# Ordering a layer's ScalarE and VectorE work behind the weight splits, and cutting the layer heads into parts

## The chip, the cores and the metric

The kernel runs on one NeuronCore of a Trainium2 chip. The metric is the device time of one execution in microseconds (us). Before the change the median of three runs is 1137.03 us (1136.1 to 1137.7).

## The reference

Two layers over a 512 x 1024 activation `x`, float32, and a last RMSNorm. Each layer normalizes `x`, projects it with one wide matrix, runs three mixers on column blocks of the result, gates and sums them, and projects back:

```python
h = rmsnorm(x, norm_g)
aq, ak, av, az, buv, bz, cq, ck, cv, cz, gl = split_cols(h @ w_in)
ya = rmsnorm(diff_attention(rope(aq), rope(ak), av, lam), subln_g) * (1 - lam_init) * silu(az)
u, vb = split(gelu(buv)); yb = u * sgu(layernorm(vb)) * silu(bz)      # chunks of 128 positions
yc = dilated_window_attention(rope(cq), rope(ck), cv) * silu(cz)      # three (window, dilation) patterns
pb = einsum('nbsc,ncd->nbsd', [ya, yb, yc], w_branch)
x = x + (sigmoid(gl) * pb).sum(branches) @ w_out
```

`lam` is a scalar of each layer, made from four short vectors (`exp(q1.k1) - exp(q2.k2) + lam_init`).

## The kernel before, in words

**Weights.** A weight is read as a unit of 128 x 1024 float32 by a DMA that SyncE issues (`load`, two `raw` buffers). Each unit is two slots of 128 x 512. A slot is split by `slot`: ScalarE copies it to the rounded type (`whi`, L159), and a subtraction gives the rest (`wlo`, L160), on VectorE, for every fifth slot after the 32nd on GpSimd. There are six `whi` and five `wlo` buffers, so a slot's split waits until the matmuls of the slot six (five) earlier are done. A product is three matmuls (`mm3`: high times high, high times low, low times high), and a slot feeds twelve of 512 columns.

Some pairs of units ("S" groups) go through a seven-product scheme instead: GpSimd and VectorE first form four sums of weight blocks (`t12`, `t34`, L179 to L182), and those are then split like weights. `t12` and `t34` share their two buffers with the probabilities `pr` of the attention.

**Activations.** `x` is split in the same way, into `xh` and `xl`, by `split` (ScalarE L402, VectorE or GpSimd L403), once the norm's scale has been put into `xf` (L555). `mixes` forms eight sums and differences of `x` blocks for the seven-product scheme (`tm`, L475 to L478) and splits them (`mh`, `ml`).

**The order of a layer** is the list of `plan`: `vb` (the gelu half of the gating unit), `val A`, `val C`, then `split`, `mix`, then `pp`, which projects pairs of blocks (q and k of a head, or z), attention A, attention C, `sgu`, the gates and branch products, and `out`. `vb`, `val A` and `val C` are the 512-wide projections (`proj_M`): eight slots each, chunk by chunk of the 1024 inputs. They use an unscaled split of `x` (`xuh`, `xul`). While they run, the head of the layer is prepared: `scale` in `i_vb` (L555, eight instructions), the gelu of `vb` (`gelu2`: L458 to L461), its statistics (L568 to L570), then `i_split` and `i_mix`.

**Banks.** `ps_pj` and `ps_s` have two PSUM banks each and `ps_to` four. A third product in `ps_pj` waits until the first has been read.

**Order on an engine.** Each engine runs its instructions strictly in the order of its queue. The queues are put in order when the program is built: a scheduler takes the instructions with their dependencies and lays them out on a simulated timeline of its own, and weight splits have a raised priority (`PRIO`). `V`, `A`, `G`, `T` are VectorE, ScalarE, GpSimd and TensorE.

Of the kernel before, what the change touches and what calls it, by code (L numbers as in the profile page):

```python
# [16 lines left out]
PSUM = bass.MemoryType.PSUM  # L17

# [13 lines left out]
XLG = (1, 3, 5, 7)  # L32
# [65 lines left out]

@with_exitstack
def hybrid_kernel(ctx: ExitStack, tc, xT, posr, wpack, tabs, cvec, pvec, rvec, lamv, sguw, outT):  # L100
# [264 lines left out]
    lambdas()  # L365
# [161 lines left out]
    def layer(l, xu, parts):  # L527
# [13 lines left out]
        def i_vb():  # L541
# [7 lines left out]
            def scale():  # L549
                bc = rms_spread(norm["rst"])  # L550
                rbc = t2k("sh", name="rbc")
                A.activation(out=rbc, in_=bc, func=AF.Copy)
                for kc in range(KC):
                    xsc = xu.f[kc // 2][:, kc % 2, :]
                    V.scalar_tensor_tensor(  # L555
                        out=xsc, in0=xsc, scalar=ng[:, l, kc : kc + 1], in1=rbc, op0=ALU.mult, op1=ALU.mult
                    )

            banks = [ps_to() for _ in range(4)]
            yield from proj_M(banks, xu.pair, {1: norm_sum, 4: scale})  # L560
            rst = norm["rst"]
            mv = sm.tile([P, 4, 2], F32, tag="mv", bufs=1, name="mv")
            rv = sm.tile([P, 4, 1], F32, tag="rv", bufs=1, name="rv")
            for tb in range(4):
                o = vb[:, tb, :]
                A.activation(out=o, in_=banks[tb], func=AF.Copy, scale=rst[:, tb : tb + 1])
                gelu2(o, o)
                V.bn_stats(out=st[:, tb, :], in_=o)  # L568
                V.bn_aggr(out=mv[:, tb, :], in_=st[:, tb : tb + 1, :])
            V.tensor_scalar(out=rv, in0=mv[:, :, 1:2], scalar1=4.0 * EPS, scalar2=None, op0=ALU.add)  # L570
            G.tensor_tensor(out=rv[:, :, 0], in0=rv[:, :, 0], in1=mhalf, op=ALU.pow)
            sgu["norm"] = mv, rv

        def i_split():
            for kc in range(KC):
                split(xh[:, kc, :], xl[:, kc, :], xu.f[kc // 2][:, kc % 2, :], G if kc in XLG else V)
            return
            yield
# [89 lines left out]
        def i_val(br):  # L668
            if br == BR_A:
                val[br] = v = new_y("va")  # L670
                banks = [ps_pj(), ps_pj(), ps_s(), ps_s()]
                yield from proj_M(banks, xu.pair, {})
# [6 lines left out]
            yield from proj_M(banks, xu.pair, {})  # L679
# [110 lines left out]
        def final(c):  # L790
# [8 lines left out]
            "vb": i_vb, "split": i_split, "mix": i_mix, "vbn": i_vbn, "after": i_after, "u2": i_u2, "bz2": i_bz2, "sgu": i_sgu, "val": i_val, "pp": i_pp, "gl2": i_gl2, "pb": i_pb, "out": i_out,  # L799
# [312 lines left out]
```

## Time and profile before

| | before |
|---|---|
| median of three runs | 1137.03 us |
| profiled execution | 1134.42 us |
| its span, first to last instruction | 1132.7 us |
| mean granted TensorE clock | 0.994 |
| TensorE (PE) busy | 1101.8 us, 97% |
| VectorE (DVE) busy | 815.2 us, 72% |
| ScalarE (ACT) busy | 598.4 us, 53% |
| GpSimd (POOL) busy | 487.8 us, 43% |
| VectorE `wlo` of `raw` (L160) | 261 instructions, mean 820 ns |
| VectorE `wlo` of `t` (L160) | 88 instructions, mean 1070 ns |

PE's busy time is close to the span, so PE sets the time wherever its queue does not wait. What is left, 1132.7 - 1101.8 = 30.9 us, is idle time of PE, at the start, in waits and at the end. The other engines are busy less, but they run in order too, and where one of them is late with something PE needs, PE waits.

### The profile page before, as it was taken

To read this page: it belongs to the slowest core of one execution; us is meant where nothing else is said; L and a number is where in the kernel's file an instruction comes from. 1 tells how busy PE (TensorE), PEld (TensorE's weight loads), DVE (VectorE), ACT (ScalarE), POOL (GpSimd) and SP (SyncE) were. 2 spreads that over 40 slices of the span, in tenths; PEclk is the share of its full clock that TensorE was granted. 3 is DMA by queue.
4 is the path that set the end of the run, shared out by engine and by line. 5 is a ranking of instruction groups with operands and counts; after the bars stand their busy time and mean duration, and the time that the engine had idled before them with its cause. 6 is when DMAs were issued, how large, how long until landed. Compare 5 with 4: busy or idle time off the path is not lost.

```text
span 1132.7 us, 17894 instructions
## 1 busy us (share of the span) xinstructions
PE 1101.8 (97%) x6444; PEld 943.7 (83%) x6444; DVE 815.2 (72%) x1500; ACT 598.4 (53%) x1281; POOL 487.8 (43%) x438
## 2 busy tenths in 40 slices
PE   7799999999998999999999999999999999999996
PEld 5588878877878999998888878788788889999886
DVE  7776777566769888874559578775679787788643
ACT  6654655566765444443546546464757644445330
POOL 4313434432524656663334235524244256657431
PEclk9999999999999999999999999999999999999998
DMA  6242221221213233333622413132203122333433
GB/s 204 73 130 93 69 82 56 93 76 38 75 38 113 89 99 97 109 115 110 223 93 75 130 38 112 39 111 76 75 3 111 56 80 91 111 112 94 138 118 98
DMA packets 35064, 105.97 MB, mean 94 GB/s; under 512 B 4704, under 2 KB 7776, under 8 KB 34976
## 3 DMA queue, kind: packets, MB, share of 16 engines
q1 hardware_dynamic: 29936, 98.50, 27.7%
q10 hardware_dynamic: 5040, 6.34, 1.8%
q8 instruction: 51, 0.84, 0.3%
q14 instruction: 37, 0.30, 0.1%
HBM read 100.58 MB, written 4.24 MB: 93 GB/s over the span
## 4 chain that ended last, share of the span: by engine, by line
PE 86%; DVE 8%; DMA 2%; issue 2%; ACT 1%; POOL 1%; POOLq 0%; SPq 0%; DVEq 0%; ACTq 0%
PE ps_pj L397 15%; PE ps_pj L398 15%; PE ps_pj L399 15%; PE ps_to L397 8%; PE ps_to L399 8%; PE ps_to L398 8%; PE ps_s L823 4%; PE ps_to L862 2%; PE ps_to L424 2%; PE ps_to L968 2%; PE ps_to L893 2%; PE ps_to L422 2%; PE ps_to L423 2%; DVE wlo L160 2%; DVE xf L555 1%
## 5 line engine op out<-in xcount | busy, mean ns | idle before, releaser
L159 ACT ACTIVATE whi<-raw 128x512 fp32r<-128x512 f32 x316 | 193.8, 627 | 254.5 <-DMA raw<-in_wpack 122.7
L160 DVE TENSOR_TENSOR wlo<-raw,whi 128x512 fp32r<-128x512 f32 x261 | 212.1, 820 | 113.9 <-ACT whi L159 36.9
L397 PE MATMUL ps_pj<-xh,whi 128*128 128x512 f32 (+1 forms) x544 | 208.5, 383 | 0.8 <-ACT whi L159 0.5
L398 PE MATMUL ps_pj<-xl,whi 128*128 128x512 f32 (+1 forms) x544 | 206.0, 379 | 0.0
L399 PE MATMUL ps_pj<-xh,wlo 128*128 128x512 f32 (+1 forms) x544 | 205.5, 378 | 0.0
L160 POOL TENSOR_TENSOR wlo<-raw,whi 128x512 fp32r<-128x512 f32 x55 | 76.8, 1397 | 139.1 <-PE ps_pj L399 53.4
L397 PEld LDWEIGHTS ps_pj<-xh,whi 128*128 128x128 f32 x544 | 102.5, 188 | 21.6 <-issue 3.6
L399 PEld LDWEIGHTS ps_pj<-xh,wlo 128*128 128x128 f32 x544 | 102.5, 188 | 19.4 <-issue 2.7
L398 PEld LDWEIGHTS ps_pj<-xl,whi 128*128 128x128 f32 x544 | 102.6, 189 | 18.4 <-issue 2.3
L160 DVE TENSOR_TENSOR wlo<-t,whi 128x512 fp32r<-128x512 f32 x88 | 92.5, 1070 | 16.1 <-ACT whi L159 9.8
L159 ACT ACTIVATE whi<-t 128x512 fp32r<-128x512 f32 x112 | 65.7, 624 | 53.8 <-DVE t L180 35.2
L397 PE MATMUL ps_to<-mh,whi 128*128 128x256 f32 x320 | 91.1, 285 | 1.4 <-DVE zs L507 0.7
L398 PE MATMUL ps_to<-ml,whi 128*128 128x256 f32 x320 | 90.5, 283 | 0.0
L399 PE MATMUL ps_to<-mh,wlo 128*128 128x256 f32 x320 | 90.1, 283 | 0.0
L838 ACT ACTIVATE pr<-pr,nm 128x128 f32<-128x128 f32 (+3 forms) x128 | 70.6, 553 | 32.9 <-DVE nm L834 32.7
L440 POOL TENSOR_TENSOR rsh<-rsh,sinr 128x512 f32<-128x512 f32 x32 | 41.8, 1307 | 105.2 <-DVE rsh L438 95.1
L834 DVE CUSTOM_DVE_ANT_0 pr<-ps_s,tab 128x128 f32<-128x128 f32 (+3 forms) x128 | 57.4, 485 | 28.6 <-PE ps_s L823 26.4
L397 PE MATMUL ps_to<-xh,whi 128*128 128x256 f32 x240 | 68.0, 283 | 0.7 <-ACT whi L159 0.7
L399 PE MATMUL ps_to<-xh,wlo 128*128 128x256 f32 x240 | 67.5, 284 | 1.0 <-DVE wlo L160 1.0
L398 PE MATMUL ps_to<-xl,whi 128*128 128x256 f32 x240 | 67.8, 283 | 0.0
L397 PEld LDWEIGHTS ps_to<-mh,whi 128*128 128x128 f32 x320 | 61.3, 192 | 3.3 <-ACT whi L159 1.6
L399 PEld LDWEIGHTS ps_to<-mh,wlo 128*128 128x128 f32 x320 | 61.1, 192 | 0.6 <-DVE wlo L160 0.4
(241 smaller groups left out, 2864.0 us busy)
## 6 DMA issues: line engine op xcount, KB each, us to landing
raw<-in_wpack SPq DMA_DIRECT2D x174, 512.0 KB
xf<-in_xT SPq DMA_DIRECT2D x8, 256.0 KB
xr<-in_xT ACTq DMA_DIRECT2D x8, 256.0 KB
x1d<-xf SPq DMA_DIRECT2D x8, 256.0 KB
raw<-in_wpack SPq DMA_DIRECT2D x4, 256.0 KB
xr<-x1d ACTq DMA_DIRECT2D x4, 256.0 KB
xr<-x1d ACTq DMA_DIRECT2D x8, 128.0 KB
out<-xf SPq DMA_DIRECT2D x8, 128.0 KB
```

Of the source, the lines that this page charges most:

```text
L159: A.activation(out=hi, in_=src, func=AF.Copy)
L160: (G if made[0] % LOMOD == 0 and made[0] > FIRST_G else V).tensor_tensor(out=lo, in0=src, in1=hi.bitcast(F32), op=ALU.subtract)
L397: T.matmul(ps, lhsT=wh, rhs=mh, start=first, stop=False)
L398: T.matmul(ps, lhsT=wh, rhs=ml, start=False, stop=False)
L399: T.matmul(ps, lhsT=wl, rhs=mh, start=False, stop=last)
L422: T.matmul(banks[tb], lhsT=mh_[:, ts], rhs=wh, start=kc == 0, stop=False)
L423: T.matmul(banks[tb], lhsT=ml_[:, ts], rhs=wh, start=False, stop=False)
L424: T.matmul(banks[tb], lhsT=mh_[:, ts], rhs=wl, start=False, stop=kc == KC - 1)
L440: G.tensor_tensor(out=sh, in0=sh, in1=sinr, op=ALU.mult)
L823: T.matmul(pss[m][:, at[i]], lhsT=q[HALF[m], a, qs], rhs=k[HALF[m], b, :W], start=t == 0, stop=t == 2)
L834: V.tensor_tensor_reduce(out=o, in0=pss[m][:, at[i]], in1=tab[:, 0 if br == BR_A else 1, S - W :], op0=ALU.add, op1=ALU.min, scale=-0.125, ...
L838: A.activation(out=o, in_=o, func=AF.Exp, scale=-1.0, bias=nm[:, m : m + 1], accum_out=den[:, m : m + 1],)
```

## The change

`V` and `A` are wrapped from the first layer on in a class, `Behind`: every ScalarE or VectorE instruction that a layer issues through them gets an ordering dependency, without a semaphore, on the newest plain weight split of its engine at the time it was written (`newest`). It must stand behind that split in the queue. The four splits of a seven-product group (`plain=False`) don't count as newest. The splits of the weights themselves are issued through `nc.scalar` and `nc.vector`.

The head is cut up. `prepare(kc)` is called after each chunk of `val A`: one `xf` scaling, and after every second chunk the gelu and statistics of one block of `vb`. `split_x(kc)` is called after each chunk of `val C`: one split of `x`, all eight now on VectorE (four were on GpSimd). `mix` comes after `val C` as before, but behind the weights. The lambdas of both layers, with their DMA, move from ahead of the layers to the end of `val C` of the first. There are six `wlo` buffers instead of five. In the last layer, three additions of squares move from GpSimd to VectorE. The instructions of TensorE are the same, and their order changes in places.

The diff, with imports and renamings left out:

```diff
-XLG = (1, 3, 5, 7)
-    start = [("vb",), ("val", BR_A), ("val", BR_C), ("split",), ("mix",), ("pp", BR_A, 0)]
+    start = [("vb",), ("val", BR_A), ("val", BR_C), ("mix",), ("pp", BR_A, 0)]
...
+class Behind:
+    def __init__(self, tc, eng, newest, n):
+        self.tc, self.eng, self.newest, self.n = tc, eng, newest, n
+    def __getattr__(self, name):
+        fn = getattr(self.eng, name)
+        def issue(*a, **k):
+            r = fn(*a, **k)
+            self.tc.add_manual_dep(r.ins, self.newest[self.n].name, ORDER, reason="behind the weights")
+            return r
+        return issue
...
+    newest = [None, None]
+    @contextmanager
+    def behind_weights():
+        with tc.issue_after(newest[0]), tc.issue_after(newest[1]):
+            yield
...
-    def slot(src, dst=None):
+    def slot(src, dst=None, plain=True):
...
-            lo = wp.tile([P, S], F32R, tag="wlo", bufs=NSLOT - 1, name="wlo")
+            lo = wp.tile([P, S], F32R, tag="wlo", bufs=NSLOT, name="wlo")
...
+            a = nc.scalar.activation(out=hi, in_=src, func=AF.Copy).ins
+            r = (G if on_g else nc.vector).tensor_tensor(out=lo, in0=src, in1=hi.bitcast(F32), op=ALU.subtract)
+            if plain and dst is None:
+                newest[0] = a
+                if not on_g:
+                    newest[1] = r.ins
...
-                        slot(src)
+                        slot(src, plain=False)
...
-                (V if kc == KC - 1 or self.first else G).tensor_tensor(out=self.ss[:, c], in0=self.ss[:, c], in1=sq[:, c], op=ALU.add)
+                (V if kc == KC - 1 or self.first or c.start else G).tensor_tensor(out=self.ss[:, c], in0=self.ss[:, c], in1=sq[:, c], op=ALU.add)
...
-    lambdas()
...
+        def prepare(kc):
+            xsc = xu.f[kc // 2][:, kc % 2, :]
+            st, mv, rv = sgu["norm"]
+            tb = kc // 2
+            o = sgu["vb"][:, tb, :]
+            with behind_weights():
+                V.scalar_tensor_tensor(
+                    out=xsc, in0=xsc, scalar=ng[:, l, kc : kc + 1], in1=norm["rbc"], op0=ALU.mult, op1=ALU.mult
+                )
+                if kc % 2:
+                    gelu2(o, o)
+                    V.bn_stats(out=st[:, tb, :], in_=o)
+                    V.bn_aggr(out=mv[:, tb, :], in_=st[:, tb : tb + 1, :])
...
+        def split_x(kc):
+            with behind_weights():
+                split(xh[:, kc, :], xl[:, kc, :], xu.f[kc // 2][:, kc % 2, :])
+                if l == 0 and kc == KC - 1:
+                    lambdas()
...
-            mixes(blocks)
+            with behind_weights():
+                mixes(blocks)
...
-                yield from proj_M(banks, xu.pair, {})
+                yield from proj_M(banks, xu.pair, {kc: partial(prepare, kc) for kc in range(KC)})
...
-            yield from proj_M(banks, xu.pair, {})
+            yield from proj_M(banks, xu.pair, {kc: partial(split_x, kc) for kc in range(KC)})
...
+    V, A = Behind(tc, nc.vector, newest, 1), Behind(tc, nc.scalar, newest, 0)
```

**Place 1, VectorE, first layer's head (`val A` runs on TensorE).** `wlo` is a weight's rest, `xf` the scaled `x`, `gw` and `vb` steps of the gelu, `st` the statistics, `xl` the rest of `x`; the numbers tell buffers' uses apart. Before:

```order
L555 SCALAR_TENSOR_TENSOR xf_98<-xf_98,pv_87,rbc_359 128x512 x2
L555 SCALAR_TENSOR_TENSOR xf_104<-xf_104,pv_87,rbc_359 128x512 x2
L555 SCALAR_TENSOR_TENSOR xf_110<-xf_110,pv_87,rbc_359 128x512 x2
L555 SCALAR_TENSOR_TENSOR xf_113<-xf_113,pv_87,rbc_359 128x512 x2
L568 BN_STATS st_257<-vb_254 128x6
L461 SCALAR_TENSOR_TENSOR vb_254<-gth_434,vb_254 128x512
L459 SCALAR_TENSOR_TENSOR gw_442<-gw_442,vb_254 128x512
L459 SCALAR_TENSOR_TENSOR gw_451<-gw_451,vb_254 128x512
L403 TENSOR_TENSOR xl_93<-xf_98,xh_92 128x512
L403 TENSOR_TENSOR xl_93<-xf_104,xh_92 128x512
L403 TENSOR_TENSOR xl_93<-xf_110,xh_92 128x512
L160 TENSOR_TENSOR wlo_416<-raw_337,whi_415 128x512
```

And now, the same stretch (L187 is the weight's subtraction, L110 the wrapper's line):

```order
L187 TENSOR_TENSOR wlo_421<-raw_361,whi_420 128x512
L110 SCALAR_TENSOR_TENSOR xf_98<-xf_98,pv_87,rbc_343 128x512
L187 TENSOR_TENSOR wlo_438<-raw_361,whi_437 128x512
L110 SCALAR_TENSOR_TENSOR xf_98<-xf_98,pv_87,rbc_343 128x512
L110 SCALAR_TENSOR_TENSOR gw_444<-gw_444,vb_238 128x512
L187 TENSOR_TENSOR wlo_465<-raw_395,whi_464 128x512
L110 SCALAR_TENSOR_TENSOR xf_104<-xf_104,pv_87,rbc_343 128x512
L187 TENSOR_TENSOR wlo_482<-raw_395,whi_481 128x512
L110 SCALAR_TENSOR_TENSOR xf_104<-xf_104,pv_87,rbc_343 128x512
L110 SCALAR_TENSOR_TENSOR gw_488<-gw_488,vb_238 128x512
L110 SCALAR_TENSOR_TENSOR vb_238<-gth_445,vb_238 128x512
L187 TENSOR_TENSOR wlo_509<-raw_441,whi_508 128x512
```

Before, fifteen instructions of the head stand together ahead of `wlo_416`. Now a `wlo` stands behind every one to three of them.

**Place 2, VectorE, from `val C` to the first `pp` of the first layer.** `vs` is the eviction of `val C`, `rsh` and `t1` are the two readers of the first `pp` bank (`ps_pj_803`), `ml` rests of the mixes, `neglam` the lambdas. Before:

```order
L160 TENSOR_TENSOR wlo_741<-raw_676,whi_740 128x512
L685 SCALAR_TENSOR_TENSOR vs_746<-ps_to_609,rp_303,vs_746 128x8x64
L160 TENSOR_TENSOR wlo_817<-raw_710,whi_816 128x512
L438 STREAM_SHUFFLE rsh_839<-ps_pj_803 128x512
L439 TENSOR_TENSOR t1_838<-ps_pj_803,cosr_125 128x512
L160 TENSOR_TENSOR wlo_833<-raw_710,whi_832 128x512
```

And now, the last twelve rows up to the same `t1`:

```order
L433 TENSOR_TENSOR ml_95<-tm_787,mh_94 128x512
L110 TENSOR_TENSOR neglam_127<-le_750 128x1 x2
L433 TENSOR_TENSOR ml_95<-tm_772,mh_94 128x512
L433 TENSOR_TENSOR ml_95<-tm_788,mh_94 128x512
L433 TENSOR_TENSOR ml_95<-tm_774,mh_94 128x512
L187 TENSOR_TENSOR wlo_833<-raw_704,whi_832 128x512
L187 TENSOR_TENSOR wlo_861<-raw_742,whi_860 128x512
L433 TENSOR_TENSOR ml_95<-tm_790,mh_94 128x512
L187 TENSOR_TENSOR wlo_877<-raw_742,whi_876 128x512
L110 TENSOR_SCALAR neglam_127<-neglam_127 128x1 x2
L110 STREAM_SHUFFLE rsh_839<-ps_pj_803 128x512
L110 TENSOR_TENSOR t1_838<-ps_pj_803,cosr_125 128x512
```

The two readers of the bank have moved behind the mixes and behind `wlo_877`. Between `wlo_739` (slot 29, counted from 0; before it has the name `wlo_741`) and the first row shown stand two `lp`, two `sg`, four `tm`, one `xl`, two `le`, three `ml`, the four `vs` and `wlo_817`. So from `wlo_739` to `t1_838` there are seventeen instructions of 128x512 (four `tm`, one `xl`, eight `ml`, four `wlo`), four `vs` and ten tiny ones. `wlo_877` is slot 33, whose buffers slot 27 had, the last that `ps_pj_847` uses; the third product, `ps_pj_891`, follows `ps_pj_847` on TensorE directly, before and now. In the second layer the same place has four `tm`, one `xl`, eight `ml`, two `wlo` and four `vs` ahead of the two readers, and no lambdas.

**Place 3, VectorE, attention C of the first layer, while the seven-product group of `t12_2808` and `t34_2809` is split.** `zs` and `ea` read the `ps_pj` banks of the products, `pr` with `nm` reads the scores in `ps_s`. Before:

```order
L507 TENSOR_TENSOR zs_3064<-ps_pj_3113,ea_3066 128x256
L403 TENSOR_TENSOR q_3061<-t1_3055,q_3061 128x512
L403 TENSOR_TENSOR ptl_2862<-ps_to_3046,pth_2861 128x128
L403 TENSOR_TENSOR ptl_2862<-ps_to_3050,pth_2861 128x2x128
L507 TENSOR_TENSOR ea_3066<-ps_pj_3151,ea_3066 128x256
L160 TENSOR_TENSOR wlo_3018<-t34_2809,whi_3017 128x512
L160 TENSOR_TENSOR wlo_3043<-t12_2808,whi_3042 128x512
L160 TENSOR_TENSOR wlo_3082<-t34_2809,whi_3081 128x512
L834 ISA pr_3000,nm_3001<-ps_s_2992,tab_91 128x384
```

And now:

```order
L433 TENSOR_TENSOR ptl_2862<-ps_to_3050,pth_2861 128x2x128
L433 TENSOR_TENSOR q_3061<-t1_3055,q_3061 128x512
L187 TENSOR_TENSOR wlo_3018<-t34_2809,whi_3017 128x512
L187 TENSOR_TENSOR wlo_3043<-t12_2808,whi_3042 128x512
L187 TENSOR_TENSOR wlo_3082<-t34_2809,whi_3081 128x512
L110 ISA pr_3000,nm_3001<-ps_s_2992,tab_91 128x384
L110 ISA nm_3001 128x1
L110 ISA pr_3000,nm_3001<-ps_s_2993,tab_91 128x384
L110 ISA nm_3001 128x1
L187 TENSOR_TENSOR wlo_3127<-raw_2917,whi_3126 128x512
L110 TENSOR_TENSOR zs_3064<-ps_pj_3113,ea_3066 128x256
```

`zs_3064` stood five instructions ahead of the three splits and now stands behind them, behind two score reads and behind `wlo_3127`, whose weights are still to be loaded. `ea_3066` now stands behind `wlo_3171`. On TensorE the same place reads before, from the last transposes of the attention on:

```order
L862 MATMUL ps_to_3050<-ident_116,pr_2879 128x128 x2
L968 MATMUL ps_to_2855<-pth_2857,vs_746 128x256
L968 MATMUL ps_to_2855<-ptl_2858,vs_746 128x256
L968 MATMUL ps_to_2855<-pth_2857,vs_746 128x256
L968 MATMUL ps_to_2855<-ptl_2858,vs_746 128x256
L397 MATMUL ps_pj_3151<-mh_94,whi_2947 128x256
L398 MATMUL ps_pj_3151<-ml_95,whi_2947 128x256
```

And now:

```order
L899 MATMUL ps_to_3050<-ident_116,pr_2879 128x128 x2
L1005 MATMUL ps_to_2855<-pth_2857,vs_762 128x256
L1005 MATMUL ps_to_2855<-ptl_2858,vs_762 128x256
L1005 MATMUL ps_to_2855<-pth_2857,vs_762 128x256
L1005 MATMUL ps_to_2855<-ptl_2858,vs_762 128x256
L1005 MATMUL ps_to_2856<-pth_2861,vs_762 128x256
L1005 MATMUL ps_to_2856<-ptl_2862,vs_762 128x256
L1005 MATMUL ps_to_2856<-pth_2861,vs_762 128x256
L1005 MATMUL ps_to_2856<-ptl_2862,vs_762 128x256
L860 MATMUL ps_s_3093<-k_2848,q_2792 128x512 x3
L860 MATMUL ps_s_3094<-k_2848,q_2792 128x512 x3
L427 MATMUL ps_pj_3151<-mh_94,whi_2947 128x256
```

The products `ps_pj_3151`, `ps_pj_3175` and `ps_pj_3202` ran before the scores `ps_s_3093`, and now run behind them. After `ps_pj_3151` come `ps_pj_3175`, six transposes of `pr_3000` and then `ps_pj_3202`, which needs the bank that `ea_3066` reads. On ScalarE, between `whi_3144` and `whi_3170`, which `wlo_3171` needs, stand four exponentials, one copy of `zs` and four scalings of the probabilities; before, two exponentials stood there. Attention C of the second layer is ordered alike.

## Rows read from the trace of the kernel before

**Rows 1.** The page: busy time of an engine, share of the span, instructions.

```profile
PE 1101.8 (97%) x6444; PEld 943.7 (83%) x6444; DVE 815.2 (72%) x1500; ACT 598.4 (53%) x1281; POOL 487.8 (43%) x438
```

**Rows 2.** Waits of PE over the whole span: total, times, longest.

```profile
PE ps_pj L424 <- DVE wlo L160: 7.5, 1, 7.5
...
PE ps_s L374 <- POOL ssum L275: 1.0, 1, 1.0
```

**Rows 3.** Timeline, DVE, first layer's head: start, length, instruction, idle before.

```profile
41.00 8.51 DVE L555 SCALAR_TENSOR_TENSOR xf<-xf,pv,rbc 128x512 f32<-128x512 f32 x8
...
51.11 3.41 DVE L459 SCALAR_TENSOR_TENSOR gw<-gw,vb 128x512 f32<-128x512 f32 x2
54.44 1.88 DVE L403 TENSOR_TENSOR xl<-xf,xh 128x512 fp32r<-128x512 f32 x3
```

**Rows 4.** Timeline, PE: behind three waits, and where full rate returns.

```profile
56.98 1.22 PE L424 MATMUL ps_pj<-wlo,xuh 128*128 128x512 f32 x2 [7.52 <-DVE wlo L160]
...
60.47 0.40 PE L422 MATMUL ps_s<-whi,xuh 128*128 128x512 f32 x1
...
365.22 0.50 PE L398 MATMUL ps_pj<-yB,whi 128*128 128x512 f32 x1 [1.84 <-DVE yB L403]
...
621.31 0.50 PE L424 MATMUL ps_to<-wlo,xuh 128*128 128x512 f32 x1 [0.40 <-DVE wlo L160]
```

**Rows 5.** Windows behind two waits: length, busy (count) by engine, PEclk, DMA.

```profile
57.00:58.80 1.80, 1.80 (x4) 1.47 (x5) 1.80 (x5) 0.00 (x0) 0.00 (x0) 0.50 0.26 59
365.20:368.00 2.80, 2.78 (x18) 2.56 (x19) 2.80 (x5) 0.24 (x1) 0.46 (x1) 1.00 0.20 82
```

**Rows 6.** Timeline, PE, where the first pp begins.

```profile
86.81 0.39 PE L397 MATMUL ps_pj<-xh,whi 128*128 128x512 f32 x1
...
87.49 0.39 PE L397 MATMUL ps_pj<-xh,whi 128*128 128x512 f32 x1
```

**Rows 7.** Timeline, DVE, around the first pp.

```profile
88.09 2.07 DVE L685 SCALAR_TENSOR_TENSOR vs<-ps_to,rp,vs 128x512 fp32r<-128x512 f32 x3 [0.33 <-ACT vs L684]
...
93.13 0.73 DVE L438 STREAM_SHUFFLE rsh<-ps_pj 128x512 f32<-128x512 f32 x1
93.76 0.67 DVE L439 TENSOR_TENSOR t<-ps_pj,cosr 128x512 f32<-128x512 f32 x1
```

**Rows 8.** Groups of DVE by line: count, busy, mean ns, idle before.

```profile
L347 DVE TENSOR_TENSOR lp<-lam_in 128x128 f32<-128x128 f32 x2 | 0.5, 278 | 0.0
```

**Rows 9.** Timeline, PE, attention C, first layer.

```profile
295.18 0.49 PE L862 MATMUL ps_to<-ident,pr 128*128 128x128 f32 x3
...
295.98 0.28 PE L397 MATMUL ps_pj<-mh,whi 128*128 128x256 f32 x1
296.10 0.28 PE L398 MATMUL ps_pj<-ml,whi 128*128 128x256 f32 x1
```

**Rows 10.** Timeline, POOL and ACT, the same stretch.

```profile
295.75 1.29 POOL L181 TENSOR_TENSOR t<-raw 128x512 f32<-128x512 f32 x1 [1.85 <-PE ps_to L862]
...
297.08 1.90 ACT L159 ACTIVATE whi<-t 128x512 fp32r<-128x512 f32 x3 [0.87 <-POOL t L181]
300.62 1.15 ACT L159 ACTIVATE whi<-raw 128x512 fp32r<-128x512 f32 x2 [1.64 <-DMA raw<-in_wpack]
301.68 0.60 ACT L838 ACTIVATE pr<-pr,nm 128x384 f32<-128x384 f32 x1
```

**Rows 11.** Timeline, DVE, the same stretch.

```profile
299.98 0.54 DVE L834 CUSTOM_DVE_ANT_0 pr<-ps_s,tab 128x384 f32<-128x384 f32 x1
...
300.46 0.54 DVE L834 CUSTOM_DVE_ANT_0 pr<-ps_s,tab 128x384 f32<-128x384 f32 x1
...
300.94 0.41 DVE L507 TENSOR_TENSOR eb<-ps_pj,ea 128x256 f32<-128x256 f32 x1
```

**Rows 12.** Timeline, PE and DVE, attention C, second layer.

```profile
846.50 0.49 PE L862 MATMUL ps_to<-ident,pr 128*128 128x128 f32 x3
...
852.04 0.56 DVE L834 CUSTOM_DVE_ANT_0 pr<-ps_s,tab 128x384 f32<-128x384 f32 x1
```

More of the change, by code (lines that the diff above doesn't have):

```diff
@@ L1 @@
 import math
-from contextlib import ExitStack
+from functools import partial
+from contextlib import ExitStack, contextmanager
 import concourse.bass as bass
@@ L17 @@
 PSUM = bass.MemoryType.PSUM
+ORDER = mybir.DependencyInfo(mybir.DependencyClass.NoSync, mybir.DependencyReason.DATA)
 P = 128
@@ L154, in slot @@
             hi = wp.tile([P, S], F32R, tag="whi", bufs=NSLOT, name="whi")
-            lo = wp.tile([P, S], F32R, tag="wlo", bufs=NSLOT - 1, name="wlo")
+            lo = wp.tile([P, S], F32R, tag="wlo", bufs=NSLOT, name="wlo")
         else:
             hi, lo = dst
+        on_g = made[0] % LOMOD == 0 and made[0] > FIRST_G
         with tc.high_priority(offset=PRIO):
-            A.activation(out=hi, in_=src, func=AF.Copy)
-            (G if made[0] % LOMOD == 0 and made[0] > FIRST_G else V).tensor_tensor(out=lo, in0=src, in1=hi.bitcast(F32), op=ALU.subtract)
+            a = nc.scalar.activation(out=hi, in_=src, func=AF.Copy).ins
[4 more added lines that the diff above has]
+                    newest[1] = r.ins
         slots.append((hi, lo))
@@ L547, in norm_sum, with spread @@
                 norm["rst"] = rms_sum([xu.ss])
-            def scale():
+            def spread():
                 bc = rms_spread(norm["rst"])
-                rbc = t2k("sh", name="rbc")
+                norm["rbc"] = rbc = t2k("sh", name="rbc")
                 A.activation(out=rbc, in_=bc, func=AF.Copy)
[L553 to L557, printed above, removed]
@@ L559, in i_vb @@
             banks = [ps_to() for _ in range(4)]
-            yield from proj_M(banks, xu.pair, {1: norm_sum, 4: scale})
-            rst = norm["rst"]
+            yield from proj_M(banks, xu.pair, {1: norm_sum, 4: spread})
             mv = sm.tile([P, 4, 2], F32, tag="mv", bufs=1, name="mv")
             rv = sm.tile([P, 4, 1], F32, tag="rv", bufs=1, name="rv")
+            sgu["norm"] = st, mv, rv
             for tb in range(4):
[L565 to L578, printed above, removed]
+                A.activation(out=vb[:, tb, :], in_=banks[tb], func=AF.Copy, scale=norm["rst"][:, tb : tb + 1])
@@ new lines, in prepare @@
+        def prepare(kc):
[11 more added lines that the diff above has]
+                    V.bn_aggr(out=mv[:, tb, :], in_=st[:, tb : tb + 1, :])
+                if kc == KC - 1:
+                    V.tensor_scalar(out=rv, in0=mv[:, :, 1:2], scalar1=4.0 * EPS, scalar2=None, op0=ALU.add)
+                    G.tensor_tensor(out=rv[:, :, 0], in0=rv[:, :, 0], in1=mhalf, op=ALU.pow)
@@ L609, in i_vbn @@
             vb = sgu["vb"]
-            mv, rv = sgu["norm"]
+            _, mv, rv = sgu["norm"]
             nb = sm.tile([P, 4], F32, tag="nb", bufs=1, name="nb")
@@ L798, in layer @@
         fns = {
-            "vb": i_vb, "split": i_split, "mix": i_mix, "vbn": i_vbn, "after": i_after, "u2": i_u2, "bz2": i_bz2, "sgu": i_sgu, "val": i_val, "pp": i_pp, "gl2": i_gl2, "pb": i_pb, "out": i_out,
+            "vb": i_vb, "mix": i_mix, "vbn": i_vbn, "after": i_after, "u2": i_u2, "bz2": i_bz2, "sgu": i_sgu, "val": i_val, "pp": i_pp, "gl2": i_gl2, "pb": i_pb, "out": i_out,
         }
```

## The prediction

> **What bounds the kernel now.** I read the page's busy times first: PE is busy for 1101.8 of 1132.7 us [rows 1], so a change that leaves TensorE's instructions as they are can only move the 30.9 us in which PE is idle. The list of PE's waits comes second [rows 2]: one wait of 7.5 us stands out, for a `wlo` of VectorE, in a weights' product of the first layer. The timeline of VectorE ahead of it tells why [rows 3]: eight `xf` scalings take 8.51 us, two `gw` 3.41, three `xl` 1.88, all in one piece, and only then comes the `wlo` that PE waits for. PE starts again at 56.98 after 7.52 us of idling [rows 4]. Its clock is then at the lower level: 0.50 of full, which is 1.2 GHz, at 57.00 to 58.80 [rows 5].
>
> The expectation must therefore weigh what that one wait gives back against the waits that the new order makes elsewhere. The profile before can show the durations for that, and the program's order the places.
>
> **What goes.** In the new order a `wlo` stands behind every one to three instructions of the head (place 1). A slot feeds PE for twelve matmuls; three matmuls take 0.68 us (86.81 to 87.49) [rows 6], so 0.227 each and 2.72 us a slot. VectorE has for one slot a `wlo`, one scaling, one gelu step and half a statistic, three and a half instructions; at 0.63 each (1.88 for three [rows 3]) that is 2.2 us, below 2.72. GpSimd has no instruction there that would slow them. So the wait of 7.52 us goes. Its slow start goes with it: from 56.98 to 60.47 [rows 4] there are eight matmuls, 3.49 us instead of 8 x 0.227 = 1.82, so 1.67 us more. The second layer's head has a wait of 0.40 us [rows 4], which I let go too. At the end PE waits 1.0 us for a GpSimd addition of squares [rows 2]; on VectorE, 128x256 takes about 0.4 [rows 11], so I take 0.4 us, between 0 and 1.0. Together 7.52 + 1.67 + 0.40 + 0.40 = 10.0 us, with 8.8 and 10.6 as ends.
>
> **What is late next: the first `pp` (place 2).** Let T0 be the end of `val C`, where PE begins `ps_pj_803`. It can run 48 matmuls, 48 x 0.227 = 10.9 us, and then needs the bank of `ps_pj_803` for `ps_pj_891`. Before, the bank was read 6.3 us after T0 (T0 is 86.81 [rows 6], the shuffle starts at 93.13 [rows 7]) and nothing waited. Now `wlo_739` comes first, which needs the buffers of the last slot of `val C`: a `whi` and a `wlo`, T0 + 1.2. Then seventeen instructions of 128x512 at 0.63 (10.7 us), four `vs` at 2.07 / 3 = 0.69 (2.8), ten tiny ones at between 0.1 and the 0.28 of `lp` [rows 8] (1.2 in all), and the shuffle and the multiplication at 0.63 and 0.67 [rows 7]. Sum: 1.2 + 10.7 + 2.8 + 1.2 + 1.3 = 17.2, against 10.9: a wait of 6.3 us. It cannot be nothing: `wlo_877`, two rows ahead of the shuffle, needs slot 27, so PE's own last matmul before `ps_pj_891`. From there a `whi`, a `wlo` and the two readers make 4 x 0.63 = 2.5 us. With GpSimd at work on the mixes, some VectorE instructions could be slow like the two `gw` (1.7 each [rows 3]); four such give 10.6 as the upper end. I take 5.5, since the first few can overlap the load's and PE's jitter at T0, and the pitch of neighbours is a little under their duration.
>
> In the second layer fifteen instructions of 128x512, four `vs` and no lambdas stand there: 1.2 + 9.5 + 2.8 + 1.3 = 14.8, minus 10.9 is 3.9. No `wlo` of the last slot stands ahead, so the lower end is 0; the upper is 7. I take 3.1, cut like the first.
>
> **Late as well: attention C (place 3).** Before, this stretch is tight but full: the transposes end at 295.18 + 0.49 = 295.67 [rows 9], free the buffer of `t34`, GpSimd forms it from 295.75, ScalarE copies it from 297.08 [rows 10], VectorE subtracts, and reads the scores at 299.98 and 300.46 [rows 11]. In that time PE ran three products and had work. Now it has only eight matmuls of 0.12 [rows 9], 0.96 us, then the next scores, which need the banks that those two reads free. The chain that leads there is the same, so the first bank is free at 299.98 + 0.54 = 300.5: a wait of 300.5 - 295.67 - 0.96 = 3.9 us. Then `ps_pj_3151` needs `zs_3064`, behind `wlo_3127`, whose `whi` starts when its load lands at 300.62 [rows 10]: `whi` until 301.2, `wlo` until 301.8, `zs` 0.41 [rows 11], so 302.2, where PE stood ready at 301.5: 0.7 us. After 24 matmuls (2.9 us, 305.1) it wants the transposes of `pr_3000` and `ps_pj_3202`. ScalarE works from 301.68 at four exponentials of 0.60 or more [rows 10], one `zs` and four scalings, some 5.2 us, then `whi_3170`, `wlo_3171` and `ea_3066` follow, 0.6 + 0.6 + 0.4: 308.5. With 0.4 us for the transposes PE waits about 3.0 us. The sum is 7.6; 0.1 us of idling was there before, so 7.5 are new. In the second layer the transposes end at 846.99 and the first score read at 852.04 + 0.56 = 852.6 [rows 12]: 852.6 - 846.99 - 0.96 = 4.6, and about 2 for the rest, since one wait of the two is shorter there: 6.5. If other work is as late as PE in these stretches, so that part of the wait is no loss, 3 in each remain; the upper ends are 9 and 8.
>
> **The clock.** A wait of 1.84 us leaves the granted clock at 1.00 (365.20 to 368.00 [rows 5], behind the wait at 365.22 [rows 4]); the one of 7.52 us brings 0.50 and costs 1.67. The new waits of 5.5, 3.9 and 4.6 us lie between. By the nearer of the two rows only the first counts: 1.7 us; the ends are 0 and four times that, 6.7.
>
> The Trainium skill, "TensorE: Matmul & The Clock Gate" (What's actually happening), says that the clock falls to the lower level once the array has been idle long enough, and comes back after a busy stretch. By that rule each of the four long waits would pay, which is the upper end just given, and a rival below; the trace bears out the two levels, and not yet where between 1.84 and 7.52 us the fall begins.
>
> **Moved at no cost.** The lambdas' load stands in SP's queue two units ahead of the weights that are needed then, so the two `lp` have it in time; `neglam` is first used in attention A. The sixth `wlo` buffer only frees VectorE earlier. Eight instead of four `xl` of a layer on VectorE are in the counts above. Elsewhere the order changes without a place I could price; I take 0, from -3 (the waits around 365 gone) to +4.
>
> **Sum.** -10.0 + 5.5 + 3.1 + 7.5 + 6.5 + 1.7 = +14.3 us. On the profiled execution, 1132.7 + 1.7 around the span = 1134.4, that gives 1148.7; the median lies 2.6 us over that execution, so 1137.0 + 14.3 = 1151.3. I forecast 1151 us.
>
> **Rivals.**
> 1. *The head's gain alone.* The waits at places 2 and 3 don't come up, because what stands ahead on VectorE runs earlier than I place it (in `val C`, where VectorE is half idle). Then 1137.0 - 10.0 = 1127 us; with the 2.5 us that `wlo_877` makes for certain, 1129.5. For it speaks that the scheduler's timeline put this order; against it that the buffers tie `wlo_739` to T0.
> 2. *Only place 2 counts.* Attention C stays full because the same chain was hidden before. Then -10.0 + 5.5 + 3.1 + 1.7 = +0.3, so 1137. Against it: PE's rows at place 3 show no other work between the transposes and the scores.
> 3. *Every long wait drops the clock,* and GpSimd slows VectorE at place 2: 14.3 + 5.0 + 4 = +23, so 1160 us. The rule cited above would give the first 5 us of it.
> 4. *The head stays late.* The scalings wait for `rbc` and the gelu for ScalarE, and PE still waits 4 us there: +18, 1155 us. The room of 0.5 us a slot speaks against it.
>
> **How the numbers follow.** Forecast 0.55 (1143 to 1158), rival 1 0.18, rival 2 0.12, rival 3 0.12, rival 4 0.03. Faster counts from 0.2%, 2.3 us, which is what a measurement of this kernel can tell from none. Rival 1 is faster; rival 2 splits into 0.03 faster, 0.06 the same and 0.03 slower; the rest is slower: 0.21, 0.07 and 0.72. The range runs from 1129 to 1163, which leaves out the better half of rival 1 and the tail of rival 3.
>
> **What would show it.** Right: no PE wait for `wlo` near 50 us; behind the eighth slot of `val C` a PE wait of some 5 us for `t1` in both layers, with VectorE busy without a gap before it; in attention C a PE wait of some 4 us ahead of scores, then one ahead of a 256-wide product, in both layers. Wrong: PE's busy share up and no wait over 3 us (rival 1), or waits at place 2 alone (rival 2). The forecast fails if VectorE reaches the shuffle by T0 + 11, or if the score reads of attention C run before the `wlo` of `t34`.

## The result

The changed kernel takes 1155.52 us (median of four runs, 1154.21 to 1156.02) against 1136.57 us, a ratio of 1.0162 with a 95% interval of 1.0149 to 1.0176: slower by 19 us. Forecast were 1151 us, with 1129 to 1163 as range.

The page of the changed kernel, busy time of PE (answers [rows 1]):

```profile
span 1153.9 us, 17824 instructions
...
PE 1106.0 (96%) x6444; PEld 949.9 (82%) x6444; DVE 815.4 (71%) x1511; ACT 598.0 (52%) x1281; POOL 478.9 (42%) x427
```

The span grew by 21.2 us: PE's idle time from 30.9 to 47.9 us (1153.9 - 1106.0), so by 17.0, and its busy time, with the same 6444 matmuls, by 4.2, since more of them ran at the lower clock.

The waits of PE in the changed kernel: total, times, longest (answers [rows 2]):

```profile
PE ps_pj L427 <- DVE t L110: 9.6, 2, 6.3
PE ps_s L860 <- DVE nm L110: 8.8, 4, 3.8
...
PE ps_to L427 <- DVE zs L110: 3.9, 5, 1.3
...
PE ps_to L1005 <- DVE ptl L433: 1.7, 1, 1.7
```

The 7.5 us for `wlo` is gone. In its place stand two waits for `t` (the first readers at the first `pp`), four for `nm` (score reads), and many small ones for readers of the seven-product scheme.

VectorE's timeline in the first layer's head (answers [rows 3]):

```profile
43.24 0.69 DVE L187 TENSOR_TENSOR wlo<-raw,whi 128x512 fp32r<-128x512 f32 x1 [3.74 <-PE ps_s L453]
43.85 0.74 DVE L110 SCALAR_TENSOR_TENSOR xf<-xf,pv,rbc 128x512 f32<-128x512 f32 x1
44.51 0.68 DVE L187 TENSOR_TENSOR wlo<-raw,whi 128x512 fp32r<-128x512 f32 x1
45.12 0.74 DVE L110 SCALAR_TENSOR_TENSOR xf<-xf,pv,rbc 128x512 f32<-128x512 f32 x1
```

The `wlo` now stand between the scalings, and a scaling takes 0.74 us, where eight in one piece took 8.51, 1.06 each. PE has no wait there; `val C` begins at 56.2 instead of 65.0, 8.8 us earlier.

PE and VectorE at the first `pp` of both layers (answers [rows 6, 7]):

```profile
93.26 0.68 DVE L187 TENSOR_TENSOR wlo<-raw,whi 128x512 fp32r<-128x512 f32 x1
...
93.99 0.71 DVE L110 STREAM_SHUFFLE rsh<-ps_pj 128x512 f32<-128x512 f32 x1
94.61 0.66 DVE L110 TENSOR_TENSOR t<-ps_pj,cosr 128x512 f32<-128x512 f32 x1
...
95.33 0.80 PE L427 MATMUL ps_pj<-xh,whi 128*128 128x512 f32 x1 [6.33 <-DVE t L110]
...
659.30 0.50 PE L427 MATMUL ps_pj<-xh,whi 128*128 128x512 f32 x1 [3.23 <-DVE t L110]
```

T0 is at 78.0 here, so `t1` ends at T0 + 17.3; the sum without the cut was 17.2.

Attention C, PE, then ScalarE and VectorE of the first layer (answers [rows 9 to 12]):

```profile
301.80 2.12 PE L860 MATMUL ps_s<-k,q 64*128 64x512 f32 x6 [3.76 <-DVE nm L110]
...
309.40 0.39 PE L427 MATMUL ps_pj<-mh,whi 128*128 128x256 f32 x1 [0.98 <-DVE ea L110]
...
866.69 2.12 PE L860 MATMUL ps_s<-k,q 64*128 64x512 f32 x6 [2.94 <-DVE nm L110]
...
307.68 1.14 ACT L186 ACTIVATE whi<-raw 128x512 fp32r<-128x512 f32 x2
...
308.93 0.42 DVE L110 TENSOR_TENSOR ea<-ps_pj,ea 128x256 f32<-128x256 f32 x1
```

PE waits 3.76 us ahead of the scores, then 0.98 ahead of `ps_pj_3202`, which `ea` holds. The scores themselves take 2.12 us instead of 0.97.

Windows of the changed kernel: length, busy (count) by engine, then PEclk (answers [rows 5]):

```profile
96.00:100.00 4.00, 4.00 (x11) 3.17 (x10) 1.05 (x2) 0.63 (x1) 4.00 (x4) 0.50 0.26 94
300.00:304.00 4.00, 2.20 (x7) 1.40 (x7) 3.87 (x12) 2.68 (x8) 1.36 (x2) 0.78 0.65 221
304.00:308.00 4.00, 4.00 (x28) 4.00 (x29) 0.90 (x4) 4.00 (x11) 0.02 (x1) 0.79 0.36 133
660.00:664.00 4.00, 4.00 (x13) 3.10 (x12) 3.28 (x5) 1.26 (x2) 3.84 (x4) 0.58 0.64 224
696.00:700.00 4.00, 2.90 (x14) 2.58 (x15) 3.60 (x17) 3.17 (x11) 0.00 (x0) 0.77 0.42 116
868.00:872.00 4.00, 4.00 (x18) 3.35 (x17) 2.07 (x8) 3.01 (x9) 0.00 (x0) 0.50 0.42 137
```

Ahead of the end, the clock falls at five waits of this trace instead of at one: at the first `pp` and in attention C of both layers, and at a wait of 1.29 us in attention A of the second. In a second trace of the changed kernel (the run "change again") it falls at the first `pp` and in attention C alone.

### The profile page after: what moved, and what is told of

Read it like the earlier page. It is cut to its first block, busy times and chain, and to the rows that moved or that the text cites. A ratio compares the mean times of both kernels' runs of the same rounds, so it can differ in the third digit from the quotient of the medians.

```text
span 1153.9 us, 17824 instructions
## 1 busy us (share of the span) xinstructions
PE 1106.0 (96%) x6444; PEld 949.9 (82%) x6444; DVE 815.4 (71%) x1511; ACT 598.0 (52%) x1281; POOL 478.9 (42%) x427
## 4 chain that ended last, share of the span: by engine, by line
PE 82%; DVE 7%; issue 3%; ACT 3%; DMA 3%; POOL 2%; POOLq 0%; DVEq 0%; SPq 0%; ACTq 0%
PE ps_pj L427 14%; PE ps_pj L428 14%; PE ps_pj L429 13%; PE ps_to L427 7%; PE ps_to L429 7%; PE ps_to L428 7%; PE ps_s L860 3%; PE ps_to L454 2%; DVE wlo L187 2%; PE ps_to L452 2%; PE ps_to L453 2%; PE ps_to L899 2%; DMA raw<-in_wpack 2%; PE ps_to L1005 1%; PE ps_to L930 1%
## 5 line engine op out<-in xcount | busy, mean ns | idle before, releaser
L187 DVE TENSOR_TENSOR wlo<-raw,whi 128x512 fp32r<-128x512 f32 x261 | 220.4, 849 | 150.4 <-ACT whi L186 142.0
L427 PE MATMUL ps_pj<-xh,whi 128*128 128x512 f32 (+1 forms) x544 | 211.0, 388 | 10.3 <-DVE t L110 9.6
L187 POOL TENSOR_TENSOR wlo<-raw,whi 128x512 fp32r<-128x512 f32 x55 | 80.5, 1463 | 147.6 <-ACT whi L186 124.2
L187 DVE TENSOR_TENSOR wlo<-t,whi 128x512 fp32r<-128x512 f32 x88 | 93.7, 1087 | 20.0 <-ACT whi L186 19.5
L110 ACT ACTIVATE pr<-pr,nm 128x128 f32<-128x128 f32 (+3 forms) x128 | 70.6, 552 | 43.7 <-DVE nm L110 43.6
L778 POOL TENSOR_TENSOR acc<-acc,zs 128x512 f32<-128x512 f32 x32 | 51.1, 1605 | 35.6 <-DVE zs L110 34.3
L110 DVE CUSTOM_DVE_ANT_0 pr<-ps_s,tab 128x128 f32<-128x128 f32 (+3 forms) x128 | 56.4, 485 | 11.7 <-PE ps_s L860 11.3
```

Of the source, the lines that this page charges most:

```text
L110: r = fn(*a, **k)
L187: r = (G if on_g else nc.vector).tensor_tensor(out=lo, in0=src, in1=hi.bitcast(F32), op=ALU.subtract)
L427: T.matmul(ps, lhsT=wh, rhs=mh, start=first, stop=False)
L778: G.tensor_tensor(out=acc[d], in0=acc[d], in1=th, op=ALU.add)
```

## The experiments

My theory after the comparison: the change has two separate costs, the mixes' place (waits at the first `pp`) and the wrapper (waits in the attentions and gates), and one gain, the head. The rival: one of them causes all.

| run | median us | ratio to before, 95% interval |
|---|---|---|
| heads only | 1132.75 | 0.9970 (0.9959 to 0.9980) |
| wrapper only | 1171.64 | 1.0315 (1.0281 to 1.0349) |
| change, mix later | 1173.97 | 1.0325 (1.0298 to 1.0353) |
| heads only, mix later | 1138.02 | 1.0026 (1.0011 to 1.0041) |
| heads only, mixes in halves | 1121.89 | 0.9882 (0.9862 to 0.9902) |
| change, seven-product readers free | 1133.64 | 0.9979 (0.9966 to 0.9993) |
| change, wait filled | 1158.81 | 1.0209 (1.0170 to 1.0248) |
| change again | 1153.49 | 1.0163 (1.0140 to 1.0186) |
| change, mixes in halves | 1151.88 | 1.0131 (1.0116 to 1.0147) |
| heads only, halves one chunk earlier | 1120.96 | 0.9861 (0.9843 to 0.9880) |
| readers free, mixes in halves | 1124.11 | 0.9887 (0.9871 to 0.9902) |

**Heads only.**

```diff
-    V, A = Behind(tc, nc.vector, newest, 1), Behind(tc, nc.scalar, newest, 0)
```

> The change without the wrapper: heads in parts behind the weights, everything else of a layer ordered as the scheduler likes. My theory, two separate losses: the heads in parts give 8.8 us back and cost the wait at the first pp in both layers (8.7 and 4.6 us with the slow clock behind it), the wrapper costs the other 16 us or so. Then 1136.6 - 8.8 + 13.3 = 1141 us, with PE waits of about 6 and 3 us for t at the first pp, and none of over 2 us in attention C. Rival, the wrapper is the cause of all: 1128 us, no wait at the first pp. Rival, the heads are the cause of all: 1155 us.

It took 1132.75 us, 8 below my number: the wrapper costs 21 to 23 us, more than I gave it. The sixth `wlo` buffer, the place of the lambdas and the additions at the end stay as in the change; none of them was tested alone. The waits at the first `pp` stay, as total 9.7 us in the waits of PE of this run, and the wait for `nm` is not in the list:

```profile
PE ps_pj L427 <- DVE t L469: 9.7, 2, 6.4
PE ps_to L452 <- ACT whi L186: 5.9, 2, 5.3
```

So in the change the first `pp` is the heads' doing and attention C the wrapper's.

**Wrapper only** (the kernel before, with `Behind`, `plain=False` and six `wlo` buffers; `scale`, `split` and `mix` as they were).

> The kernel before with the wrapper and six wlo buffers, heads in one piece. My theory: the wait of 7.5 us at the head stays, no wait at the first pp, and the wrapper's own costs come: attention C some 5 us in each layer, attention A and the gates 2 to 3 each, so 1136.6 + 16 = 1152 us. Rival, the wrapper is the cause of all: 1136.6 + 8.8 + 19 = 1164 us. Rival, the wrapper costs nothing without the heads in parts: 1137 us.

1171.64 us: 36 over before, every number of mine too low. The wait of 7.5 us at the head, which I expected to stay, is gone in this run too. The eight scalings still stand in one piece:

```profile
42.47 5.39 DVE L110 SCALAR_TENSOR_TENSOR xf<-xf,pv,rbc 128x512 f32<-128x512 f32 x8
```

They take 5.39 us instead of 8.51, the `xl` no longer stand between them and the next `wlo`, and `val C` begins at 56.2, as in the change. So either part alone takes the head's wait away; that the cutting is needed for it is not shown. PE also waits at the first `pp` (3.66 and 4.13 us), and in each layer 2.35 for `xl` behind the head: the last `xl` of the first layer stand behind the weight splits of `val C` and come from 81.5 us on, where PE has begun the first `pp` at 79.2. The two parts are not additive.

**Change, mix later; heads only, mix later.**

```diff
-("val", BR_C), ("mix",), ("pp", BR_A, 0)]
+("val", BR_C), ("pp", BR_A, 0), ("mix",)]
```

> The changed kernel with mix listed behind the first pp instead of ahead of it, so that twelve of the seventeen instructions of 128x512 leave the stretch ahead of the first readers. My theory: both waits at the first pp go with the slow clock behind them, 8.7 + 4.6 us, unless the mixes make their readers late: 1155.5 - 13 = 1142 us, attention C as before this edit. Rival, the weight splits ahead of the readers hold them, not the mixes: the waits shrink to about 2.5 us and the time to about 1148 us.

> Heads in parts, no wrapper, mix behind the first pp. My theory, the two losses are separate and add: 1141 - 13 = 1128 us, the head's gain kept whole, PE waits over 1.5 us nowhere but at the start and the end. Rival, the mixes only move the wait on to the second pp or the first scores: 1133 to 1137 us, with a PE wait for t or nm of 3 us or more near 95 to 115 us.

The first was far worse than either number (1173.97, some 20 over the change). The second came out about as its rival had it: 1138.02, 5 over heads only, with waits for `k` and `z` (2.45 and 1.56 us at 102 and 104 us) where the rival had named `t` or `nm`. PE's timeline of the first run:

```profile
104.33 0.86 PE L860 MATMUL ps_s<-k,q 64*128 64x128 f32 x10 [3.88 <-DVE k L433]
107.33 0.80 PE L427 MATMUL ps_pj<-xh,whi 128*128 128x512 f32 x1 [2.15 <-DVE z L110]
...
681.89 0.79 PE L427 MATMUL ps_pj<-xh,whi 128*128 128x512 f32 x1 [4.31 <-DVE z L110]
```

The wait for `t` is gone, but the mixes now stand ahead of the last step of `k` and of the reader `z`, and PE waits there. Moved backwards, VectorE's work only changes whom it holds up.

**Heads only, mixes in halves.** Moved forwards instead, into `val C`:

```diff
+MIXAT = (1, 4)
...
-("val", BR_C), ("mix",), ("pp", BR_A, 0)]
+("val", BR_C), ("pp", BR_A, 0)]
...
                 split(xh[:, kc, :], xl[:, kc, :], xu.f[kc // 2][:, kc % 2, :])
+                if kc in MIXAT:
+                    mixes(mix_blocks, (MIXAT.index(kc),))
```

> Heads in parts, no wrapper, and the mixes made in two halves inside val C (behind its second and fifth chunk) instead of behind it, so that only four vs and two wlo stand ahead of the first readers. My theory, the mixes' place made the waits at the first pp (6.4 and 3.3 us in the heads-only run, each with a slow clock behind it): they go, 1132.8 - 14 = 1119 us. Rival, VectorE is too full in val C with them: weight splits late there, PE waits for wlo of 1 us and more near 60 to 78 us, 1128 us or more. Rival, the wait only moves to k and z as in the run with mix behind the first pp: 1133 us or more.

1121.89 us, 10.9 below heads only (10.0 by the ratios in the table; the two ran on different chips), of 14 expected. PE's one wait at the first `pp` of the first layer:

```profile
90.85 0.50 PE L428 MATMUL ps_pj<-xh,whi 128*128 128x512 f32 x1 [2.38 <-DVE t L470]
```

2.38 us are left of 6.4, and the second layer's wait is gone. No `wlo` is late in `val C`.

**Change, seven-product readers free.**

```diff
-        def add(out, ps, o, e=V):
+        def add(out, ps, o, e=nc.vector):
...
-        A.activation(out=e1, in_=p, func=AF.Copy)
+        nc.scalar.activation(out=e1, in_=p, func=AF.Copy)
...
-        A.activation(out=z2[:, LT], in_=p, func=AF.Copy)
+        nc.scalar.activation(out=z2[:, LT], in_=p, func=AF.Copy)
```

> The changed kernel with the readers of the seven-product scheme (zs, ea, eb) taken out of the wrapper, all else in it. My theory, what the wrapper costs is mostly that these readers stand behind weight splits: the waits for nm, ea and zs in attention C, some 9 us with the clock, and for zs and ea in the gates, 5 us, go: 1155.5 - 14 = 1141 us, still some 8 over the heads-only run. Rival, the wrapper's cost lies in the attention's own instructions (scores, exponentials): 1152 us or more.

1133.64 us: 20 below the change run on the same chip, so within 1 us of heads only, all that the wrapper costs. The waits of PE in this run:

```profile
PE ps_pj L427 <- DVE t L110: 9.6, 2, 6.3
...
PE ps_pj L428 <- DVE y L433: 3.2, 4, 1.9
```

The waits for `nm` are gone, those for `zs` and `ea` down to 0.5 us in all, and the waits at the first `pp` are the same. New are 3.2 us of waits for `y`, an input of the branch products. In this kernel the wrapper's constraint on the readers of the seven-product groups makes up its whole cost within 1 us; on all other instructions it costs nothing that shows in the time.

**Change, wait filled; change again.**

```diff
+            if l == 0 and (br, i) == (BR_A, 0):
+                fill = ps_to()
+                for n in range(24):
+                    T.matmul(fill, lhsT=xh[:, n % KC, 0:P], rhs=xh[:, n % KC, :], start=n == 0, stop=n == 23)
```

> The changed kernel with 24 more matmuls of 128x512 (5.4 us at full rate) into an unused bank ahead of the third product of the first layer, so that PE is busy in most of the wait at the first pp. VectorE's work is the same, so the third product starts at the same time. My theory, the slow stretch behind the wait comes from PE's idling and goes: 1155.5 - 2.4 = 1153 us, granted clock 1.00 at 95 to 104 us. Rival, PE is slow there for another reason (its operands, the banks): no change, 1155.5 us, or 1161 if the matmuls add to the path.

> The changed kernel once more, unchanged, on the same chip as the two runs that edit it: 1155.5 us by either theory.

The window behind the wait, in the filled run:

```profile
96.00:100.00 4.00, 4.00 (x20) 3.29 (x19) 1.03 (x2) 1.42 (x3) 4.00 (x5) 1.00 0.29 118
```

The clock stays at 1.00, where it is 0.50 in the change: idling makes this slow stretch. The time is not 2.4 us shorter, though. Its median is 5 us longer, but the four runs reach from 1154.89 to 1164.91 and the intervals in the table overlap, so that it is longer is not certain. The next wait on PE, of the filled run and of the change again:

```profile
132.60 1.57 PE L864 MATMUL ps_s<-k,q 64*128 64x384 f32 x6 [2.15 <-DVE nm L110]
```

```profile
132.59 1.14 PE L860 MATMUL ps_s<-k,q 64*128 64x384 f32 x6 [0.78 <-DVE nm L110]
```

PE comes to it 1.4 us earlier and goes on at the same time, and the scores then take 1.57 us instead of 1.14: the clock falls there instead (0.63 at 132 to 136 us, 1.00 in the change again). The 24 matmuls also made the scheduler order later places otherwise, so the rest of the difference is not separated.

**Change, mixes in halves** (the edit above, with the wrapper).

> The changed kernel, wrapper and all, with the mixes in two halves inside val C. It takes the first pp's wait alone out of the change. My theory, the wait at the first pp and the wrapper's cost on the seven-product readers are separate: the heads-only run gained 10.9 us by this edit (1132.8 to 1121.9), so 1154 - 11 = 1143 us, waits for nm in attention C of 3 to 4 us as before the edit. Rival, the two are one (what PE saves at the first pp is lost again at the readers further on, as in the run with filled wait): 1150 us or more.

1151.88 us, 1.6 below the change again (3.6 by the ratios; the two ran on different chips), of 11 expected: the rival, 1150 us or more. PE's timeline:

```profile
127.15 1.67 PE L857 MATMUL ps_s<-k,q 64*128 64x384 f32 x6 [3.08 <-DVE nm L111]
...
352.96 0.58 PE L428 MATMUL ps_pj<-mh,whi 128*128 128x256 f32 x1 [3.25 <-ACT zs L111]
```

There is no wait for `t`. But the waits at attention A (3.08 instead of 0.78) and at `zs` (3.25 instead of 0.92) grow by 4.6 us. PE's start times of the same matmuls in this run and in the change again show the rest, the clock included: PE is 8.6 us ahead behind the first `pp` (102.02 against 110.65), 3.7 behind the first scores of attention A (138.13 against 141.87) and level at 382 us (382.04 against 381.96). In the second layer it gains 5 us at the first `pp` and keeps some of them. So with the wrapper the two costs are not separate: in the first layer PE loses all that it saves at the first `pp` again at the readers behind it.

**The two versions for use.** Halves behind the first and fourth chunk (`MIXAT = (0, 3)`), without the wrapper; and halves behind the second and fifth (`(1, 4)`), with the wrapper but for the seven-product readers.

> Heads in parts, no wrapper, the mixes' halves one chunk earlier, behind the first and fourth chunk of val C; one weight split less then stands ahead of the first readers. My theory: the 2.4 us wait left there (t, at 91 us) shrinks by the one wlo and the backlog behind it, 1121.9 - 2 = 1120 us. Rival, VectorE's backlog in val C is the same and the wait stays: 1122 us.

> The changed kernel with the wrapper everywhere but on the seven-product readers, and the mixes in halves: what the rest of the wrapper is worth. My theory, nothing: 1122 us, as without any wrapper. Rival, the wrapper keeps weight splits in time elsewhere: 1117 us or less. Rival, it costs in the attention's own instructions: 1126 us or more.

1120.96 us, the lowest median, 1.4% below the kernel before, and not told apart from the 1121.89 of `(1, 4)`; and 1124.11 us, so the rest of the wrapper is worth nothing, or costs up to some 2 us. Waits of PE in the fastest run:

```profile
PE ps_to L453 <- ACT whi L187: 5.3, 1, 5.3
...
PE ps_pj L428 <- DVE zs L538: 1.5, 2, 0.9
...
PE ps_pj L428 <- DVE t L470: 0.2, 1, 0.2
```

The longest is the start. Of the wait for `t` 0.2 us is left.

## Why the prediction was right, point by point

- **The head:** right in place and size, sized 7.52 + 1.67 + 0.40. The wait of 7.52 us and its slow stretch went, and `val C` begins 8.8 us earlier, though PE had lost 0.6 at the start (16.93 against 16.34). That GpSimd has no instruction there was not quite so: one `tm` ran from 53.99 to 55.67, and a `wlo` that began at 55.11 took 1.11 us, without a wait of PE. Why the wait went is less sure than I wrote, since the wrapper alone removed it too.
- **The first `pp`:** right in place, cause and size: 6.33 and 3.23 us against 5.5 and 3.1. The uncut 6.3 for the first layer was the better number. That the mixes' place causes it, the run with halves shows.
- **Attention C:** the mechanism was right, and the terms of 7.5 and 6.5 us too large as waits. In the first layer the wait ahead of the scores was 3.76 (3.9 forecast) and the one for `ea` 0.98 (3.0 forecast). In the second layer the 4.6 forecast ahead of the scores came in two pieces, 1.67 for `ptl` and 2.94 for `nm`. The others, 0.7 for `zs` and about 2 in the second layer, did not come, because PE, at the lower clock, reached those places late: the scores took 2.12 us. In the first layer PE ran 4.25 us of work (six scores at 0.97, 24 matmuls, the transposes at 0.4) between about 297.9 and 309.40: 7.3 us lost, 4.74 of them as waits. Against the kernel before it is less. PE's start times of one matmul ahead of this stretch and one behind it, before (first two rows; the earlier one is in [rows 9]) and now:

```profile
295.18 0.49 PE L862 MATMUL ps_to<-ident,pr 128*128 128x128 f32 x3
...
339.55 0.28 PE L397 MATMUL ps_pj<-xh,whi 128*128 128x256 f32 x1
...
295.99 0.49 PE L899 MATMUL ps_to<-ident,pr 128*128 128x128 f32 x3
...
346.05 0.28 PE L427 MATMUL ps_pj<-xh,whi 128*128 128x256 f32 x1
```

  The changed kernel is 0.81 us late ahead of it and 6.50 behind it, so attention C cost 5.7 us, with the clock. In the second layer the same reading gives 5.7 again (13.60 late, then 19.26).
- **The clock:** mis-sized. I let it fall behind one wait; it fell at five in this trace and at four in the other trace of the same kernel. PE's busy time grew by 4.2 us, where my terms, 1.7 added and 1.67 gone, made about 0. "By the nearer of the two rows" failed: 3.23 us is nearer to the wait that left the clock at 1.00 and brought 0.58, and so are 3.76 and 2.94.
- **"Elsewhere I take 0":** this step failed. PE's timeline at places I gave no price:

```profile
133.44 1.14 PE L860 MATMUL ps_s<-k,q 64*128 64x384 f32 x6 [0.76 <-DVE nm L110]
...
442.80 0.39 PE L427 MATMUL ps_to<-mh,whi 128*128 128x256 f32 x1 [1.30 <-DVE zs L110]
...
696.95 1.13 PE L860 MATMUL ps_s<-k,q 64*128 64x384 f32 x6 [1.29 <-DVE nm L110]
```

  Attention A costs 3.0 us of waits in both layers together (0.5 before), and the gates have eight waits of 0.5 to 1.3 us for readers of the seven-product scheme. It is the same mechanism as at place 3, in every such group; I priced it in two of them.
- **The tail:** no gain, where I took 0.4. The additions on VectorE stand behind its last `xf`:

```profile
1143.25 0.42 DVE L110 SCALAR_TENSOR_TENSOR xf<-ps_to,xr 128x256 f32<-128x256 f32 x1 [0.63 <-PE ps_to L429]
1143.59 0.42 DVE L110 TENSOR_TENSOR ssum<-ssum,sq 128x256 f32<-128x256 f32 x1
...
1144.15 0.35 PE L404 MATMUL ps_s<-ones,ssum 128*128 128x1 f32 x2 [0.94 <-DVE ssum L110]
```

- **Rival 1** is refuted for the change as it is, and true of its head: with the wrapper off and the mixes forward, 1121 us. **Rival 2** is refuted by the waits in attention C, **rival 4** by PE's having no wait at the head. **Rival 3** came true in its first half: the long waits all dropped the clock. By the rule of the Trainium skill cited there ("TensorE: Matmul & The Clock Gate", What's actually happening) that was to be expected. The trace agrees for the long waits: 0.50 and 0.58 behind waits of 6.33 and 3.23 us. Why a wait of 1.29 us dropped the clock too, no run here shows.

So +19 us against +14.3 forecast comes about by attention C too large, the clock and the unpriced groups too small. By PE's start times of the same matmuls, in the two profiles, whose spans differ by 21.2 us, the first `pp` cost 9.2 and 5.2 us (forecast with its clock 10.3 in all), attention C 5.7 and 5.7 (14.0), and what lies elsewhere some 5 (0); the heads gave 10.0 (9.6). The errors have both signs, so the total came nearer by luck than its parts did. That the forecast's parts can be added was itself wrong: the run with halves in the changed kernel saves the 9.6 us of waits at the first `pp` and keeps 1.6 to 3.6.

## What to carry to other kernels

In this kernel an order that puts every instruction behind the newest prefetched weight makes readers wait for buffers that PE itself has still to free, or for loads; leave out whatever frees a bank PE needs next. Work that has to make room is moved forward into a stretch where its engine idles, not behind, where it holds up the next reader. Where an engine in order paces several places, a wait taken away at one of them is worth only what the next places let through: measure the parts together.

## What the runs showed of the hardware that I had not expected

The lower clock does not go by the length of the wait alone, nor by the kernel and the place. Behind a wait of 1.29 us at 696.95 the changed kernel's clock is 0.77 at 696 to 700. The second trace of the same kernel has the same order on every engine and nearly the same wait there, and the clock stays at 1.00:

```profile
696.01 1.13 PE L860 MATMUL ps_s<-k,q 64*128 64x384 f32 x6 [1.28 <-DVE nm L110]
...
696.00:700.00 4.00, 3.84 (x28) 3.52 (x29) 3.62 (x12) 3.47 (x13) 0.03 (x1) 1.00 0.28 63
```

What PE did just ahead of the wait does not tell the two apart either. In the three microseconds up to the wait's end it was busy for 1.71 us in the first trace and 1.73 in the second:

```profile
694.00:697.00 3.00, 1.71 (x16) 1.52 (x14) 2.85 (x9) 1.24 (x3) 1.59 (x1) 1.00 0.83 303
...
693.00:696.00 3.00, 1.73 (x15) 1.53 (x14) 2.85 (x9) 1.30 (x3) 1.60 (x1) 1.00 0.85 313
```

Other runs agree that the length does not decide. The wait of 1.84 us for `yB` [rows 4] left the clock at 1.00 [rows 5]. In the run "heads only, mix later" PE waits 1.83 us at the same place, and the clock falls to 0.50. In the run "heads only, mixes in halves" a wait of 2.38 us left it at 1.00. The windows behind these last two:

```profile
364.00:367.00 3.00, 3.00 (x15) 2.90 (x14) 3.00 (x6) 0.17 (x1) 0.00 (x0) 0.50 0.00 0
...
91.00:95.00 4.00, 4.00 (x18) 3.31 (x19) 4.00 (x5) 1.15 (x2) 3.84 (x4) 1.00 0.31 117
```

All waits of 2.94 us and more that come after the start dropped it in the changed kernel's two traces. For shorter ones no run here shows what decides.

And a slow stretch can hide a wait: at half rate PE reached the next reader late enough that the reader was done (in attention C 7.3 us were lost and 4.74 listed as waits), so the list of waits shows less than was lost.
